# Softmax probabilities: turned by the vector engine and a trip through DRAM in place of the tensor engine, with the consumers of turned results begun later

## The chip, the cores and the metric

The kernel runs on one core of a Trainium2 chip. The core has a matrix engine (PE in the profile, with its weight loads listed apart as PEld), a vector engine (DVE), a scalar engine (ACT), GpSimd (POOL), and a queue engine, SyncE (SP), which here issues nearly every transfer between DRAM and the core's own memory (SBUF). Matrix results land in a small accumulator memory (PSUM) of eight banks. The metric is the device time of one execution in microseconds (us); the figure for a kernel is the median of several runs.

## The reference

One encoder layer on 256 tokens of width 2048, in float32, cut to what matters here:

```python
u = rmsnorm(h, norm_mix_g)
z = u @ w_in                      # split into b_a, c_a, v_a, q, k, v, gl_a, gl_b
y_a = (b_a * centred_dwconv3(c_a * v_a, conv_a_w)) @ w_out_a
q, k = rope(q), rope(k)           # 16 query heads, 4 key/value heads, head size 64
# window of +-128 tokens, one sink logit per head:
m = max(max(scores), sink); p = exp(scores - m)
p = p / (sum(p) + exp(sink - m))
y_b = (p @ v).reshape(b, s, D_ATTN) @ w_o_attn
h = h + (sigmoid(gl_a + b_a') * y_a + sigmoid(gl_b + b_b') * y_b) @ w_mix_out
up = centred_dwconv3(rmsnorm(h, norm_ffn_g) @ ffn_w_up, ffn_conv_w) + ffn_conv_b
h = h + (silu(up[..., :5632]) * up[..., 5632:]) @ ffn_w_down
out = rmsnorm(h, norm_final_g)
```

## The kernel before

**Products.** Each large product is made from rounded halves: a weight tile `raw` is cast to a high part `whi` by ACT (line 195), the rest `wlo` is a subtraction on DVE (line 206), and PE sums high and low products into one PSUM bank. The weights come in chunks of 512 KB. A product is of one of two kinds. A *single* job (lines 253 and 254) has the weights standing still and the tokens moving, and its result has features on the partitions, as the rest of the kernel wants it; a chunk is eight pairs of a 512-column and a 256-column matmul. A *quad* job (lines 229 to 231) has the tokens standing still and 512 weight columns moving, and its result has tokens on the partitions. It must be turned. `quad` (line 300) does it without PE: two DVE transposes of 32 x 32 blocks (line 310, one for each half of the tokens) into `qd`, one DMA of 512 KB to a DRAM buffer `way` (line 314), four DMAs of 128 KB back into `qf` (line 317), and then four consumers, one for each 128 features, on `qf`.

**Order of the work.** Nothing is scheduled automatically: the program order on each engine is the order in which the Python code issues. `run` walks over the chunks. At chunk c it issues the fetch of chunk c+6, the cast of chunk c+3, the subtraction of chunk c+2 and then the matmuls of chunk c; then one *step* follows. In a step every generator under way is resumed once up to its next `yield`, in the order in which they were begun, and after that the work due at this step begins (`at(n, fn)`, `later`). So a `yield 1` means "the rest is issued one chunk later", and the DVE work of the step at c stands between the subtractions of chunks c+1 and c+2. Each engine runs its own queue strictly in order, so an instruction that waits holds up all behind it. There are three `wlo` buffers, so DVE can be at most that far ahead of PE.

**Stages.** First the wide start and the single jobs of `w_in` (keys, values, queries, then the short convolution), up to about 231 us; then quad jobs for the gates, `w_oa` and `w_o` (8 pairs of rows each, so four chunks a quad), and `w_mix` (the first two of its four quads side by side). These quads live in pool `p1b`, and the code calls their setting `stage1`. Then `w_up` and `w_dn` follow in `stage2`, and four single jobs end the kernel.

**Attention** lies inside the single jobs of `w_in`, in ten blocks t = 0 to 9, at steps 29 + 21t/4. Block t issues `att_out(t - 2)`, `att_turn(t - 1, e)` for e = 0 and 1, and `att_scores(t, e)`, each as far as the first `yield`. `att_scores` puts the scores of a head for both blocks of 128 queries into banks `s0` and `s1` on PE; DVE adds the mask and takes the maximum; one step later ACT takes the exponentials into `p`; one step later DVE makes the denominator and ACT scales `p`. `att_turn` turns `p` (queries on the partitions) by four PE transposes into bank `ptp` (line 565) and, a step later, ACT copies that to `pT` (line 568). `att_out` multiplies the values `vtok` by `pT` into bank `av` (line 578). Up to block 1 the queries' rotation is also under way: `rope` moves halves with four DMAs `rot<-qkraw` (line 473) and four DMAs `two<-rcos` (line 485), all on the SP queue. `rcos` has one buffer, so the next `rcos` on DVE (line 475) waits until those DMAs have read the last one.

**Turned pairs.** `turns(which)` lets some pairs of a single job run low before high. `BEHIND` says which pairs after an attention block.

Of the kernel before, what the change touches and what calls it, by code (L numbers as in the profile page):

```python
# [7 lines left out]
F32 = mybir.dt.float32  # L8
F32R = mybir.dt.float32r
# [11 lines left out]
HD = 64  # L21
# [31 lines left out]
def hybrid_block_kernel(  # L53
    ctx: ExitStack, tc: tile.TileContext, head, wide, xT, w_in, w_gate, w_oa, w_o, w_mix, w_up, w_dn, w_end, vec, cst, out
):
    nc = tc.nc
# [4 lines left out]
    turn = ctx.enter_context(tc.tile_pool(name="turn", bufs=2, space=bass.MemoryType.DRAM))  # L61
    lin = ctx.enter_context(tc.tile_pool(name="lin", bufs=3, space=PSUM))
    aps = ctx.enter_context(tc.tile_pool(name="aps", bufs=1, space=PSUM))

    x = cpool.tile([P, KT, T], F32, tag="x", name="x")
# [55 lines left out]

    TURNS, BEHIND = (1, 5, 9, 15), {"s": (1, 5), "ptp": (1, 5), "av": (1, 4)}
    pairs = [0]
    order = {"due": None, "turned": set()}

    def turns(which=TURNS):
        order["due"], order["turned"] = which, set()
# [162 lines left out]
    S = 32  # L292

    def by_block_of_tokens(a):

        return a.rearrange("p (h a i) -> p h a i", h=2, a=4)

    under_way = [0]

    def quad(*epis, stage, bufs):  # L300
        def go(banks):
            while under_way[0] >= bufs:
                yield 1
            under_way[0] += 1
            pool = stage()
            d = pool.tile([P, 4, 2, QUAD * S], F32, tag="qd", name="qd", bufs=bufs)
            for h, ps in enumerate(banks):
                if h:
                    yield 1
                nc.vector.transpose(d[:, :, h, :], ps)  # L310
            f = pool.tile([P, 4, 2, QUAD, S], F32, tag="qf", name="qf", bufs=bufs)

            way = turn.tile([4, S, 4, 2 * QUAD * S], F32, tag="way", name="way")
            nc.sync.dma_start(way.rearrange("a j b x -> (a j) (b x)"), d.rearrange("p b h x -> p (b h x)"))
            yield 1
            for b in range(4):
                nc.sync.dma_start(  # L317
                    f[S * b : S * b + S].rearrange("p a h m i -> p a (h m i)"),
                    way[:, :, b, :].rearrange("a j x -> j a x"),
                )  # L320
            for _ in range(2):
                yield 1
            for m, epi in enumerate(epis):
                begin(epi, f[:, :, :, m, :].rearrange("p a h i -> p h a i"))
                if m < 2:
                    yield 1
            under_way[0] -= 1

        return go
# [49 lines left out]
    hd = p1.tile([P, HEAD], F32, tag="hd", name="hd")  # L379
    ct = p1.tile([P, C_END], F32, tag="ct", name="ct")  # L380
    ident = ct[:, C_ID : C_ID + P]
    hb = p1.tile([P, WIDE, P], F32, tag="hb", name="hb")


    wm = p1.tile([P, 2 * T], F32R, tag="wm", name="wm")
    nc.vector.memset(wm.bitcast(F32), 1.0)
    nc.vector.memset(ones, 1.0 / D)
    nc.vector.memset(eps, EPS)
    xs = cpool.tile([P, KT, 2 * T], F32R, tag="A", name="xs")
# [134 lines left out]
        yield 1  # L524
        nc.scalar.copy(vtok[:, :, i * P : (i + 1) * P], tp[:, :, 0:P])

    probs = {}
    mask = ct[:, C_MASK : C_MASK + T]

    def att_scores(t, e):  # L530
        kv = t // 4
        sc = aps.tile([P, 2, T], F32, tag=f"s{e}", name=f"s{e}")
        for n in range(2):
            q = qs[:, t // 2, e, t % 2, n * P : (n + 1) * P]
            nc.tensor.matmul(sc[:, n, :], q, kh[:, e, kv, :], start=True, stop=False)  # L535
            nc.tensor.matmul(sc[:, n, :], q, kl[:, e, kv, :], start=False, stop=True)  # L536
        h = PAIRS[t][e]
        sink, ns = col(V_SINK + h), nsink[:, h : h + 1]
        flat = sc.rearrange("p n t -> p (n t)")

        nc.vector.tensor_tensor(flat[:, P : 3 * P], flat[:, P : 3 * P], mask, op=ALU.add)
        st = p1.tile([P, 8], F32, tag="st", name="st", bufs=4)
        mx, nm, den, es = (st[:, 2 * i : 2 * i + 2] for i in range(4))
        nc.vector.tensor_reduce(mx, sc, axis=AX.X, op=ALU.max, negate=True)
        nc.vector.tensor_scalar(nm, mx, HD**-0.5, ns, op0=ALU.mult, op1=ALU.min)
        yield 1
        p = p1.tile([P, 2, T], F32, tag="p", name="p", bufs=3)
        for n in range(2):
            nc.scalar.activation(
                p[:, n, :], sc[:, n, :], AF.Exp, bias=nm[:, n : n + 1], scale=HD**-0.5, accum_out=den[:, n : n + 1]  # L550
            )
        nc.scalar.activation(es, nm, AF.Exp, bias=sink)
        yield 1
        nc.vector.tensor_tensor(den, den, es, op=ALU.add)
        nc.vector.reciprocal(den, den)
        for n in range(2):
            nc.scalar.mul(p[:, n, :], p[:, n, :], den[:, n : n + 1])
        probs[t, e] = p

    def att_turn(t, e):  # L560
        p = probs.pop((t, e))
        tp = aps.tile([P, 2, T], F32, tag=("tp", "tp2")[e], name="ptp")
        for b in range(2):
            for n in range(2):
                nc.tensor.transpose(tp[:, b, n * P : (n + 1) * P], p[:, n, b * P : (b + 1) * P], ident)  # L565
        yield 1
        pT = p1.tile([P, 2, T], F32, tag="pT", name="pT", bufs=2)
        nc.scalar.copy(pT, tp)
        probs[t, e] = pT

    def att_out(t):
        kv = t // 4
        o = aps.tile([P, 2 * T], F32, tag="av", name="av")
        pT = [probs.pop((t, e)) for e in range(2)]
        for b in range(2):
            for e in range(2):
                v0 = 128 * kv + 64 * e
                nc.tensor.matmul(  # L578
                    o[64 * e : 64 * e + 64, 0:T], vtok[:, b, v0 : v0 + HD], pT[e][:, b, :], start=b == 0, stop=b == 1
                )  # L580
        yield 1
        yield from split(box["B"][:, 8 + t, :], o[:, 0:T])
# [65 lines left out]
    for i in range(4):  # L648
        at(40 + 4 * i, lambda i=i: nc.sync.dma_start(x[:, 4 * i : 4 * i + 4, :], xT[:, 4 * i : 4 * i + 4, :]))


    for t in range(10):

        def block(t=t):
            if t > 1:
                begin(att_out, t - 2)
            for e in range(2):
                if 0 < t < 9:
                    begin(att_turn, t - 1, e)
            for e in range(2):  # L660
                if t < 8:
                    begin(att_scores, t, e)
            if t:
                turns(BEHIND["s" if t < 8 else "ptp" if t < 9 else "av"])

        at(29 + 21 * t // 4, block)

# [4 lines left out]
    stage1 = lambda: lazy("p1b", start_gates)  # L672
# [35 lines left out]
    def quads(w, n, rhs, epi, stage, tiles, side=1):  # L708

        jobs = []  # L710
        for q in range(len(tiles) // QUAD):
            four = [lambda f, t=t: epi(t, f) for t in tiles[QUAD * q : QUAD * q + QUAD]]
            jobs.append((w[q], n, rhs, quad(*four, stage=stage, bufs=2 if stage is stage1 else 1), "quad"))
        groups.append((2, jobs[:side], None))
        groups.extend((2, [job], None) for job in jobs[side:])

# [256 lines left out]
```

## Time and profile before

| | |
|---|---|
| median of 3 runs | 1321.75 us (1321.44 to 1321.79) |
| the profiled execution's own time | 1320.97 us |
| its span, first to last instruction | 1319.2 us |
| mean granted PE clock | 0.997 |
| PE busy | 1304.1 us, 99% of the span |
| DVE busy | 941.7 us, 71% |
| ACT busy | 678.9 us, 51% |
| POOL busy | 62.5 us, 5% |
| bytes by the DMA queues | 302.54 MB, 229 GB/s |

A row of instructions names its line, engine, operation and tiles (`ptp<-ct,p` writes `ptp` from `ct` and `p`), then the count after an x, and durations. Durations of matmuls overlap, since they are pipelined: what a matmul costs the path is the time from its start to the start of the next one. In a timeline the first number is the start in us, the second the duration, and a bracket at the end gives the engine's idle time just before and what ended it.

### The profile page before, as it was taken

What the parts mean: (1) busy time and instruction counts of PE and PEld (TensorE: products, weight loads), DVE (VectorE), ACT (ScalarE), POOL (GpSimd) and SP (SyncE); (2) the same over time, 40 slices, a digit from 0 to 9 for tenths busy, and PEclk for the clock granted to TensorE, in tenths of its full rate; (3) what the DMA queues carried; (4) which work ended last, traced back from release to release, by engine and by line L of the source; (5) the groups of instructions that cost most, each with busy time, mean ns of one, the idle gap of its engine ahead of it and who ended that gap; (6) DMA issues with size and microseconds to landing.
All of it is one profiled execution on the core that took longest, in us unless ns stands there. A gap on an engine that the chain in (4) does not pass through costs nothing.

```text
span 1319.2 us, 17559 instructions
## 1 busy us (share of the span) xinstructions
PE 1304.1 (99%) x6206; PEld 1090.2 (83%) x6206; DVE 941.7 (71%) x1390; ACT 678.9 (51%) x971; POOL 62.5 (5%) x66
## 2 busy tenths in 40 slices
PE   9999999999999999999999999999999999999997
PEld 8888888888888877878888888888888888888886
DVE  7888777555556677687798887878787875545454
ACT  7666675454444344444565555555555554434352
POOL 0000000000000000242000000000000000102031
PEclk9999999999999999999999999999999999999999
DMA  8786655677777878767776867776767676767663
GB/s 301 233 247 206 207 158 164 195 250 244 236 249 247 276 259 262 236 206 240 247 248 223 273 224 256 228 264 223 255 228 256 228 256 197 222 194 224 195 212 104
DMA packets 105032, 302.54 MB, mean 229 GB/s; under 512 B 12016, under 2 KB 35440, under 8 KB 104944
## 3 DMA queue, kind: packets, MB, share of 16 engines
q1 hardware_dynamic: 104512, 300.64, 70.7%
q8 instruction: 48, 0.79, 0.2%
q10 hardware_dynamic: 432, 0.79, 0.2%
q14 instruction: 40, 0.33, 0.1%
HBM read 271.76 MB, written 25.69 MB: 225 GB/s over the span
## 4 chain that ended last, share of the span: by engine, by line
PE 94%; DMA 3%; DVE 2%; issue 1%; SPq 0%; ACT 0%; POOLq 0%; DVEq 0%; ACTq 0%
PE pq L231 24%; PE pq L230 24%; PE pq L229 24%; PE ps L253 13%; PE ps L254 7%; DMA qf<-way 1%; DMA way<-qd 1%; DVE wlo L206 1%; PE av L578 1%; PE ptp L565 1%; SPq L317 0%; PE warm L393 0%; DVE qd L310 0%; PE s L536 0%; PE s L535 0%
## 5 line engine op out<-in xcount | busy, mean ns | idle before, releaser
L195 ACT CAST whi<-raw 128x1024 fp32r<-128x1024 f32 (+3 forms) x465 | 482.5, 1040 | 496.6 <-PE pq L230 372.9
L206 DVE TENSOR_TENSOR wlo<-raw,whi 128x1024 fp32r<-128x1024 f32 (+3 forms) x465 | 563.0, 1214 | 239.5 <-PE pq L231 134.4
L229 PE MATMUL pq<-whi,hs 128*128 128x512 f32 x704 | 274.0, 389 | 0.0
L231 PE MATMUL pq<-wlo,hs 128*128 128x512 f32 x704 | 273.9, 389 | 0.0
L230 PE MATMUL pq<-whi,hs 128*128 128x512 f32 x704 | 273.9, 389 | 0.0
L253 PE MATMUL ps<-xs,whi 128*128 128x512 f32 x576 | 200.3, 394 | 0.0
L254 PE MATMUL ps<-xs,wlo 128*128 128x256 f32 x576 | 158.0, 280 | 0.0
L229 PEld LDWEIGHTS pq<-whi,hs 128*128 128x128 f32 x704 | 132.1, 188 | 27.6
L230 PEld LDWEIGHTS pq<-whi,hs 128*128 128x128 f32 x704 | 132.1, 188 | 27.4
L231 PEld LDWEIGHTS pq<-wlo,hs 128*128 128x128 f32 x704 | 132.1, 188 | 27.3
L253 PEld LDWEIGHTS ps<-xs,whi 128*128 128x128 f32 x576 | 106.8, 188 | 22.3
L254 PEld LDWEIGHTS ps<-xs,wlo 128*128 128x128 f32 x576 | 108.9, 189 | 1.9
L229 PE MATMUL pq<-whi,xs 128*128 128x512 f32 x256 | 99.7, 390 | 0.0
L230 PE MATMUL pq<-whi,xs 128*128 128x512 f32 x256 | 99.6, 389 | 0.0
L231 PE MATMUL pq<-wlo,xs 128*128 128x512 f32 x256 | 99.6, 389 | 0.0
L458 DVE TENSOR_TENSOR evs<-qf,r 128x256 f32<-128x256 f32 x120 | 48.0, 421 | 41.8 <-DMA qf<-way 41.7
L310 DVE STREAM_TRANSPOSE qd<-pq 128x512 f32<-128x512 f32 x90 | 63.8, 709 | 9.6 <-PE pq L231 9.5
L229 PE MATMUL pq<-whi,actC 128*128 128x512 f32 x168 | 65.4, 389 | 0.0
L230 PE MATMUL pq<-whi,actC 128*128 128x512 f32 x168 | 65.4, 389 | 0.0
L231 PE MATMUL pq<-wlo,actC 128*128 128x512 f32 x168 | 65.4, 389 | 0.0
L229 PEld LDWEIGHTS pq<-whi,xs 128*128 128x128 f32 x256 | 48.0, 188 | 10.4 <-issue 0.4
L230 PEld LDWEIGHTS pq<-whi,xs 128*128 128x128 f32 x256 | 48.0, 188 | 10.0
(170 smaller groups left out, 1629.1 us busy)
## 6 DMA issues: line engine op xcount, KB each, us to landing
raw<-in_w_up_dram SPq DMA_DIRECT2D x176, 512.0 KB, 4.6
raw<-in_w_dn_dram SPq DMA_DIRECT2D x66, 512.0 KB, 4.3
raw<-in_w_gate_dram SPq DMA_DIRECT2D x64, 512.0 KB, 4.3
raw<-in_w_in_dram SPq DMA_DIRECT2D x60, 512.0 KB, 4.5
way<-qd SPq DMA_DIRECT2D x45, 512.0 KB, 2.9
qf<-way SPq DMA_DIRECT2D x180, 128.0 KB, 2.9
raw<-in_w_mix_dram SPq DMA_DIRECT2D x32, 512.0 KB, 4.5
raw<-in_w_end_dram SPq DMA_DIRECT2D x20, 512.0 KB, 3.7
```

Of the source, the lines that this page charges most:

```text
L195: nc.scalar.copy(his[c][:, a:b, :], raws[c](a, b))
L206: nc.vector.tensor_tensor(los[c][:, a:b, :], raw(a, b), his[c][:, a:b, :], op=ALU.subtract)
L229: nc.tensor.matmul(ps, ah, wh, start=k == 0, stop=False)
L230: nc.tensor.matmul(ps, al, wh, start=False, stop=False)
L231: nc.tensor.matmul(ps, ah, wl, start=False, stop=last)
L253: lambda: nc.tensor.matmul(both, hi[:, i, :], moving, start=k == 0, stop=last and turned),
L254: lambda: nc.tensor.matmul(ps[:, 0:T], lo[:, i, :], a[:, 0:T], start=False, stop=last and not turned),
L310: nc.vector.transpose(d[:, :, h, :], ps)
L458: nc.vector.tensor_tensor(by_block_of_tokens(dst), f, by_block_of_tokens(rr["r"]), op=ALU.mult)
L565: nc.tensor.transpose(tp[:, b, n * P : (n + 1) * P], p[:, n, b * P : (b + 1) * P], ident)
L578: nc.tensor.matmul(o[64 * e : 64 * e + 64, 0:T], vtok[:, b, v0 : v0 + HD], pT[e][:, b, :], start=b == 0, stop=b == 1)
```

## The change

Four things change; the numbers of matmuls and of weight bytes stay.

1. `att_turn` goes. In `att_scores`, a step after `p` is scaled, DVE turns its 32 x 32 blocks into a tile `pd` (for both heads of block t, four instructions of 128 x 256); then, as in `quad`, one DMA of 512 KB goes to `way` and, a step later, four DMAs of 128 KB come back into `pT`. `att_out` reads `pT` with runs of 32 elements. The trip that `quad` had inline is now the function `by_dram` that both use.
2. `quad` waits a number of steps between the reads and the first consumer: it was 2 everywhere, and is 4 in `stage1` (with 3 buffers in place of 2) and 3 in `stage2`.
3. The turned pairs: block 0 gets `TURNS`, block 1 none, block 8 the setting of "av".
4. To make room, `hb` shares the place of `pd` and the warm-up tile that of `p`, and `p` has two buffers, not three.

```diff
-    TURNS, BEHIND = (1, 5, 9, 15), {"s": (1, 5), "ptp": (1, 5), "av": (1, 4)}
+    TURNS, BEHIND = (1, 5, 9, 15), {"s": (1, 5), "av": (1, 4)}
...
+    def by_dram(dst, src):
+        way = turn.tile([4, S, 4, src.shape[-1] // 4], F32, tag="way", name="way")
+        nc.sync.dma_start(way.rearrange("a j b x -> (a j) (b x)"), src)
+        yield 1
+        for b in range(4):
+            nc.sync.dma_start(dst[S * b : S * b + S], way[:, :, b, :].rearrange("a j x -> j a x"))
...
-    def quad(*epis, stage, bufs):
+    def quad(*epis, stage, bufs, wait):
...
-            for _ in range(2):
+            yield from by_dram(f.rearrange("p a h m i -> p a (h m i)"), d.rearrange("p b h x -> p (b h x)"))
+            for _ in range(wait):
                 yield 1
...
-        p = p1.tile([P, 2, T], F32, tag="p", name="p", bufs=3)
+        p = p1.tile([P, 2, T], F32, tag="p", name="p", bufs=2)
...
-        probs[t, e] = p
-    def att_turn(t, e):
-        p = probs.pop((t, e))
-        tp = aps.tile([P, 2, T], F32, tag=("tp", "tp2")[e], name="ptp")
-        for b in range(2):
-            for n in range(2):
-                nc.tensor.transpose(tp[:, b, n * P : (n + 1) * P], p[:, n, b * P : (b + 1) * P], ident)
-        yield 1
-        pT = p1.tile([P, 2, T], F32, tag="pT", name="pT", bufs=2)
-        nc.scalar.copy(pT, tp)
-        probs[t, e] = pT
+        yield 1
+        if e == 0:
+            d = p1.tile([P, CH, P], F32, tag="pd", name="pd").rearrange("p k f -> p (k f)")
+            trips[t] = d.rearrange("p (b e n k i) -> p b e n k i", b=4, e=2, n=2, k=2)
+        d = trips[t]
+        for n in range(2):
+            nc.vector.transpose(d[:, :, e, n].rearrange("p b k i -> p k b i"), p[:, n, :])
+        if e == 0:
+            return
+        f = p1.tile([P, 4, 2, 2, 2, S], F32, tag="pT", name="pT", bufs=2)
+        yield from by_dram(f.rearrange("p a e n k i -> p a (e n k i)"), d.rearrange("p b e n k i -> p (b e n k i)"))
+        probs[t] = f
...
             for e in range(2):
-                if 0 < t < 9:
-                    begin(att_turn, t - 1, e)
-            for e in range(2):
                 if t < 8:
                     begin(att_scores, t, e)
-            if t:
-                turns(BEHIND["s" if t < 8 else "ptp" if t < 9 else "av"])
+            if t != 1:
+                turns(BEHIND["s" if t < 8 else "av"] if t else TURNS)
...
+        flow = {"bufs": 3, "wait": 4} if stage is stage1 else {"bufs": 1, "wait": 3}
...
-            jobs.append((w[q], n, rhs, quad(*four, stage=stage, bufs=2 if stage is stage1 else 1), "quad"))
+            jobs.append((w[q], n, rhs, quad(*four, stage=stage, **flow), "quad"))
```

Three places in the programs show what moves. On PE, at block 2, the end of one chunk, then the block: `av` the attention product, `ptp` the transposes, `s` the scores, and the next chunk of a single job. Before:

```order
L253 MATMUL ps<-xs,whi 128x512
L254 MATMUL ps<-xs,wlo 128x256
L578 MATMUL av<-pT,vtok 64x256 x4
L565 MATMUL ptp<-ct,p 128x128 x8
L535 MATMUL s_1305<-kh,qs 128x256
L536 MATMUL s_1305<-kl,qs 128x256
```

After, at the same place:

```order
L253 MATMUL ps<-xs,whi 128x512
L254 MATMUL ps<-xs,wlo 128x256
L584 MATMUL av<-pT,vtok 64x256 x4
L540 MATMUL s_1305<-kh,qs 128x256
L541 MATMUL s_1305<-kl,qs 128x256
```

The eight `ptp` rows are gone and nothing stands in their place.

On SP, around blocks 0 and 1, where the last two rotations of queries are under way (`raw` is a weight chunk). Before:

```order
L180 DMA raw<-in_w_in_dram 128x1024 x3
L485 DMA two<-rcos 64x512 x4
L180 DMA raw<-in_w_in_dram 128x1024
L473 DMA rot<-qkraw 32x512 x4
L180 DMA raw<-in_w_in_dram 128x1024 x3
L485 DMA two<-rcos 64x512 x4
```

After:

```order
L180 DMA raw<-in_w_in_dram 128x1024 x2
L304 DMA way<-pd 128x1024
L180 DMA raw<-in_w_in_dram 128x1024
L490 DMA two<-rcos 64x512 x4
L307 DMA pT<-way 32x4x256 x4
L180 DMA raw<-in_w_in_dram 128x1024
L478 DMA rot<-qkraw 32x512 x4
L180 DMA raw<-in_w_in_dram 128x1024 x3
L490 DMA two<-rcos 64x512 x4
```

The trip's write and one weight fetch now stand ahead of `two<-rcos`, and the trip's four reads ahead of `rot<-qkraw`. On DVE the four transposes of block 0 stand right before them, behind the sum that `two<-rcos` carries away.

On DVE, in `w_mix`, where the results of the first two quads are added to `x` and split into `hs` (`qd` is the drain of a quad's banks). Before:

```order
L206 TENSOR_TENSOR wlo<-raw,whi 128x1024 x2
L699 TENSOR_TENSOR x<-x,qf 128x256
L206 TENSOR_TENSOR wlo<-raw,whi 128x1024
L699 TENSOR_TENSOR x<-x,qf 128x256 x2
L206 TENSOR_TENSOR wlo<-raw,whi 128x1024
L699 TENSOR_TENSOR x<-x,qf 128x256 x3
L279 SCALAR_TENSOR_TENSOR hs<-x,vt,hs 128x256
L206 TENSOR_TENSOR wlo<-raw,whi 128x1024
L699 TENSOR_TENSOR x<-x,qf 128x256 x2
L279 SCALAR_TENSOR_TENSOR hs<-x,vt,hs 128x256 x2
L206 TENSOR_TENSOR wlo<-raw,whi 128x1024
```

After:

```order
L206 TENSOR_TENSOR wlo<-raw,whi 128x1024 x4
L701 TENSOR_TENSOR x<-x,qf 128x256
L206 TENSOR_TENSOR wlo<-raw,whi 128x1024
L701 TENSOR_TENSOR x<-x,qf 128x256 x2
L206 TENSOR_TENSOR wlo<-raw,whi 128x1024
L701 TENSOR_TENSOR x<-x,qf 128x256 x3
L279 SCALAR_TENSOR_TENSOR hs<-x,vt,hs 128x256
L206 TENSOR_TENSOR wlo<-raw,whi 128x1024
L701 TENSOR_TENSOR x<-x,qf 128x256 x2
L279 SCALAR_TENSOR_TENSOR hs<-x,vt,hs 128x256 x2
L321 STREAM_TRANSPOSE qd<-pq 128x4x128
L206 TENSOR_TENSOR wlo<-raw,whi 128x1024
```

The first addition stands two subtractions later, and the drain of the third quad now falls inside the group.

More of the change, by code (lines that the diff above doesn't have):

```diff
@@ L311, in go @@
             f = pool.tile([P, 4, 2, QUAD, S], F32, tag="qf", name="qf", bufs=bufs)
-            way = turn.tile([4, S, 4, 2 * QUAD * S], F32, tag="way", name="way")
-            nc.sync.dma_start(way.rearrange("a j b x -> (a j) (b x)"), d.rearrange("p b h x -> p (b h x)"))
-            yield 1
[L316 to L320, printed above, removed]
-            for _ in range(2):
+            yield from by_dram(f.rearrange("p a h m i -> p a (h m i)"), d.rearrange("p b h x -> p (b h x)"))
+            for _ in range(wait):
                 yield 1
@@ L381, in hybrid_block_kernel @@
     ident = ct[:, C_ID : C_ID + P]
-    hb = p1.tile([P, WIDE, P], F32, tag="hb", name="hb")
-    wm = p1.tile([P, 2 * T], F32R, tag="wm", name="wm")
-    nc.vector.memset(wm.bitcast(F32), 1.0)
+    hb = p1.tile([P, CH, P], F32, tag="pd", name="hb")[:, 0:WIDE, :]
+    wm = p1.tile([P, 2, T], F32, tag="p", name="wm", bufs=2).rearrange("p n t -> p (n t)")
+    nc.vector.memset(wm, 1.0)
+    wm = wm.bitcast(F32R)
     nc.vector.memset(ones, 1.0 / D)
@@ L525, in epi_v @@
         nc.scalar.copy(vtok[:, :, i * P : (i + 1) * P], tp[:, :, 0:P])
-    probs = {}
+    probs, trips = {}, {}
     mask = ct[:, C_MASK : C_MASK + T]
@@ L573, in att_out @@
         o = aps.tile([P, 2 * T], F32, tag="av", name="av")
-        pT = [probs.pop((t, e)) for e in range(2)]
+        pT = probs.pop(t).rearrange("p a e n k i -> p e k n a i")
         for b in range(2):
@@ L578, in att_out @@
                 nc.tensor.matmul(
-                    o[64 * e : 64 * e + 64, 0:T], vtok[:, b, v0 : v0 + HD], pT[e][:, b, :], start=b == 0, stop=b == 1
+                    o[64 * e : 64 * e + 64, 0:T], vtok[:, b, v0 : v0 + HD], pT[:, e, b], start=b == 0, stop=b == 1
                 )
```

## The prediction

> **What bounds the kernel now.** I read the page's busy shares and the chain that ended last first, then busy time by stretches, then the waits, then timelines of the places that the change touches.
>
> ```profile
> PE 1304.1 (99%) x6206; PEld 1090.2 (83%) x6206; DVE 941.7 (71%) x1390; ACT 678.9 (51%) x971; POOL 62.5 (5%) x66
> ...
> PE 94%; DMA 3%; DVE 2%; issue 1%; SPq 0%; ACT 0%; POOLq 0%; DVEq 0%; ACTq 0%
> ```
>
> PE is busy nearly throughout and is 94% of the chain. So work taken from PE shortens the kernel, work given to others is free while they keep ahead, and the only other thing to win is time in which PE waits. Where does it wait? Busy time by stretches, PE alone (first the stretch and its length, then PE busy and its instructions, the granted clock, DMA share, GB/s):
>
> ```profile
> 475.00:570.00 95.00, 90.06 (x382) 0.98 0.72 236
> 570.00:1220.00 650.00, 650.00 (x2869) 1.00 0.73 236
> ```
>
> From 570 to 1220 us a matmul takes 650/2869 = 0.2266 us and PE never stops. From 475 to 570 us 382 of them should take 86.6 us and take 95.0: 8.4 us are lost there, in `w_o` and `w_mix`. The waits tell to what:
>
> ```profile
> PE pq L231 <- DVE wlo L206: 4.9, 5, 1.9
> ...
> PEld pq L231 <- DVE wlo L206: 8.2, 9, 2.3
> ...
> DVE gates L690 <- DMA qf<-way: 10.3, 4, 4.3
> ...
> DVE x L699 <- DMA qf<-way: 10.6, 3, 3.9
> ...
> DVE evs L458 <- DMA qf<-way: 41.7, 28, 3.9
> ```
>
> PE waits for `wlo`, and DVE makes it late because it stands in front of a consumer whose `qf` has not landed. The 41.7 us of the last row belong to gates and `w_up`, where DVE has room and PE does not wait.
>
> **Part A, the PE transposes go.** Blocks 1 and 2 on PE:
>
> ```profile
> 92.14 1.04 PE L565 MATMUL ptp<-ct,p 128*128 128x128 f32 x8
> ...
> 92.93 0.36 PE L535 MATMUL s<-kh,qs 128*128 128x256 f32 x1
> ...
> 107.97 1.08 PE L578 MATMUL av<-pT,vtok 128*64 128x256 f32 x8
> 108.98 1.09 PE L565 MATMUL ptp<-ct,p 128*128 128x128 f32 x8
> 109.83 0.36 PE L535 MATMUL s<-kh,qs 128*128 128x256 f32 x1
> ```
>
> Start to start, the eight transposes cost 0.79 us in block 1 and 0.85 us in block 2; blocks 3 to 8 have the same eight. 0.79 + 7 x 0.85 = 6.7 us on the path. The slower first matmul of another type (0.36 us) stays where `av` comes before, so I count nothing for it.
>
> ```profile
> L565 PE MATMUL ptp<-ct,p x64: 272/273/329, 92.1 to 216.7; 128*128 128x128 f32 x64
> ```
>
> The Trainium skill, "TensorE: Matmul & The Clock Gate", Part 4 (PE-mode transpose), gives about 275 ns for a transpose in a kernel; the row's 273 ns agrees as a duration. Taken as a price it would make 64 x 0.273 = 17.5 us; the starts above say 0.106 each, and they decide.
>
> The 16 ACT copies go too; ACT is not waited for there, so that is worth nothing.
>
> **Part B, the turned pairs.** Chunk starts after block 0, and after block 1:
>
> ```profile
> 83.66 0.40 PE L253 MATMUL ps<-xs,whi 128*128 128x512 f32 x1
> ...
> 86.49 0.40 PE L253 MATMUL ps<-xs,whi 128*128 128x512 f32 x1
> ...
> 99.55 0.39 PE L253 MATMUL ps<-xs,whi 128*128 128x512 f32 x1
> ...
> 102.33 0.39 PE L253 MATMUL ps<-xs,whi 128*128 128x512 f32 x1
> ```
>
> Eight pairs take 2.83 us where no pair was turned after a block, 2.78 us where some were. Block 0 now gets turns, block 1 loses them: 5 chunks x 0.05 = 0.25 us won and the like lost. I take 0, ends plus and minus 0.3.
>
> **Part C, DVE and SP get the turning.** A transpose of 128 x 256 from SBUF is not in the trace; the nearest is twice the size, from PSUM:
>
> ```profile
> L310 DVE STREAM_TRANSPOSE qd<-pq 128x512 f32<-128x512 f32 x90 | 63.8, 709 | 9.6 <-PE pq L231 9.5
> ...
> way<-qd SPq DMA_DIRECT2D x45, 512.0 KB, 2.9
> qf<-way SPq DMA_DIRECT2D x180, 128.0 KB, 2.9
> ...
> 144.50:161.40 16.90, 13.05 (x26) 1.00 0.51 170
> 161.40:178.30 16.90, 12.88 (x26) 1.00 0.55 179
> ```
>
> Half of 709 ns: about 0.36 us, 1.45 us for the four of a block; ends 0.36 (size alone) and 0.71 (the writes go in runs of 32). From block 3 on (the last two rows are DVE's busy time) DVE idles 3.9 to 4.0 us a block, so this is covered, even with a block 0.85 us shorter. The trip takes 2.9 + four issues + 2.9 us, under 10 us. It starts three steps after the scores and its user comes ten steps after them, over 16 us later, so PE does not wait for `pT`. Its 8 MB are 3% more bytes, in a stage where the DMA engines are half busy.
>
> The place without room is 88 to 123 us, where the rotation of queries is under way. DVE and SP there, and PE's need for chunk 38's and 43's `wlo`:
>
> ```profile
> 87.94 0.69 DVE L481 TENSOR_TENSOR rcos<-rcos,rot 128x512 f32<-128x512 f32 x1
> ...
> 93.04 0.76 DVE L475 TENSOR_TENSOR rcos<-qkraw,ct 128x256 f32<-128x256 f32 x2 [1.80 <-DMA two<-rcos]
> ...
> 96.36 1.22 DVE L206 TENSOR_TENSOR wlo<-raw,whi 128x1024 fp32r<-128x1024 f32 x1
> ...
> 103.24 1.22 DVE L206 TENSOR_TENSOR wlo<-raw,whi 128x1024 fp32r<-128x1024 f32 x1
> ...
> 110.59 0.43 DVE L541 TENSOR_TENSOR s<-s,ct 128x256 f32<-128x256 f32 x1 [0.56 <-PE s L536]
> ...
> 119.97 1.22 DVE L206 TENSOR_TENSOR wlo<-raw,whi 128x1024 fp32r<-128x1024 f32 x1
> ...
> 88.70 2.43 SPq L485 DMA_DIRECT2D two<-rcos  x4
> ...
> 105.10 0.39 PE L253 MATMUL ps<-xs,whi 128*128 128x512 f32 x1
> ...
> 122.23 0.28 PE L254 MATMUL ps<-xs,wlo 128*128 128x256 f32 x1
> ```
>
> DVE waits 1.80 us until `two<-rcos` has read `rcos`. That DMA starts at 88.70, when the sum is done. Now the four transposes (1.45), then the issue of `way` and of a weight chunk (about 0.8) come in front: it starts near 90.95, so the next `rcos` starts at 95.3, not 93.04, and all DVE work behind it is 2.25 us late. Queued behind: the mask of block 1 and `wlo` of chunk 36, ready at 99.8 (97.58 + 2.25), while PE, 0.79 us earlier by part A, wants it at 99.0 (99.55 + 0.23 - 0.79). PE waits 0.9. Chunk 38: ready 106.7, wanted at 105.33 + 0.1: another 1.3. Block 1's own transposes then add 1.45, against idle time of 0.56 and some on ACT; chunk 43 is ready near 123.4 (121.19 + 2.3) and wanted at 122.8 (block 2 is 0.85 shorter): another 0.7. Sum 2.9 us lost. After that DVE waits for PE before block 3 and is level again. Bounds: if `two<-rcos` is not held up, the 1.80 us cover the transposes of block 0, and only chunk 43 is late: 0.8. If the DMA also lands a microsecond later behind the two transfers of 512 KB ahead of it: 5.
>
> **Part D, consumers begin later.** In `w_o`, DVE alone:
>
> ```profile
> 475.00:516.00 41.00, 34.55 (x62) 1.00 0.77 258
> ```
>
> Of 41.0 us DVE works 34.55; the other 6.45 it mostly waits for `qf`. Two more steps are 5.4 us and more than the longest of these waits, 4.3. Without them its work fits, and PE's losses there go. In `w_mix` both first quads end together, and their results come in one burst:
>
> ```profile
> 554.48 0.43 DVE L699 TENSOR_TENSOR x<-x,qf 128x256 f32<-128x256 f32 x1 [3.86 <-DMA qf<-way]
> ...
> 559.23 1.63 DVE L206 TENSOR_TENSOR wlo<-raw,whi 128x1024 fp32r<-128x1024 f32 x1
> ...
> 564.04 1.75 DVE L206 TENSOR_TENSOR wlo<-raw,whi 128x1024 fp32r<-128x1024 f32 x1
> ...
> 560.92 0.50 PE L231 MATMUL pq<-wlo,ms 128*128 128x512 f32 x1 [0.62 <-DVE wlo L206]
> ...
> 565.85 0.50 PE L231 MATMUL pq<-wlo,ms 128*128 128x512 f32 x1 [1.92 <-DVE wlo L206]
> ...
> 567.35 0.63 PE L229 MATMUL pq<-whi,ms 128*128 128x512 f32 x1
> ```
>
> DVE loses 3.86 us, then PE 0.62 and 1.92, then several matmuls run at half speed (0.63 us long). Without the wait DVE could begin the burst about 3 us earlier (the three `wlo` buffers hold it back), which covers the 2.54; but two drains of 0.71 us now fall into the burst. So I leave 1.8 us lost, ends 0 and 3.9 (2.54 + 1.4). Part D wins 8.4 - 1.8 = 6.6.
>
> "TensorE: Matmul & The Clock Gate" of the Trainium skill, Why this matters for your kernels, has the clock fall back only after idle gaps over some 3 us. Here it fell after 0.62 and 1.92; by that rule what is left costs its own length alone, by the trace it may bring slow matmuls again.
>
> In `stage2` three steps for two change nothing on PE: it never waits there (650.00 of 650.00), and a quad under way for seven steps still ends before the next one, eight chunks later. More buffers and shared places cost nothing: the sharers are used at the start, tens of us apart.
>
> **The sum.** -6.7 + 0 + 2.9 - 6.6 = -10.4 us on the profiled execution's 1320.97 us: 1310.6. The median of the runs stands 0.8 above that execution, so 1311.3. Less than 0.2% (2.6 us) could not be told from no change.
>
> **The rivals.**
> - *Attention is not held up.* For it: the 1.80 us idle, and ACT freed of its copies. Against it: SP's order. C is 0.8 and the burst fits: 1307.4 to 1309.2.
> - *The stalls at 475 to 570 us are DVE's work, not its wait.* For it: `w_o` keeps DVE 84% busy, and the burst is work. Then D wins 1.5, and 1316.4 comes out. Against it: PE's losses follow the rows that wait for `qf`.
> - *`av` slows on `pT`'s runs of 32.* No row has such a moving operand, so nothing excludes it. `av` takes 1.01 us a block start to start (107.97 to 108.98), some 0.85 of it streaming; at half speed eight blocks cost 6.8 more: 1318.1. Against it: nothing in the trace but that contiguous operands of all sizes run at one rate.
> - *Slower: DVE becomes the bound of the attention.* The transposes write in runs of 32. Cover is 4.0 - 0.85 = 3.15 us a block; to eat A and D (13.3) the loss must be 1.7 a block, so four transposes of 4.9 us, 1.2 each. At 1.6 each: 8 x (6.4 - 3.15) = 26, and 1334. Against it: 0.71 for twice the size.
>
> That the change does not take place is ruled out: the rows `ptp` are gone from PE's order.
>
> **How the numbers follow.** My forecast 45% (1308.5 to 1314 by the bounds of C and D); first rival 23%, second 14%, third 8%, slower 4%; 6% for mixtures, such as pairs in the slow order after every block (8 x 0.25 = 2 us). The range 1307 to 1317 leaves out some of the first rival, the third and the fourth: 2 in 10. Faster 0.91 (all but the last rival and a worse third one), same 0.05, slower 0.04.
>
> **What would show it.** A: no `ptp`, and `av` followed by `s` after about 1.0 us. C: `rcos` waiting for `two<-rcos` until about 95, PE waiting for `wlo` near 99, 105 and 122. D: the waits of DVE for `qf` under 10 us in all, PE without gaps from 475 to 550 us, at most 4 us lost near 560. It is wrong if a transpose of DVE takes over 0.7 us, if `av` grows, or if PE still waits in `w_o`.

## The result, and the profile after

| | before | changed |
|---|---|---|
| median | 1321.60 us (1319.94 to 1321.79, 4 runs) | 1313.84 us (1312.64 to 1313.97, 4 runs) |
| ratio | | 0.9942, 95% interval 0.9925 to 0.9959 |
| profiled execution | 1320.97 us, span 1319.2 us | 1313.97 us, span 1312.1 us |

The row of the kernel before has one run more than the table ahead of the prediction. The kernel became 0.6% faster: 7.8 us by the medians, 7.0 us between the two profiled executions. That is the forecast's direction, inside its range, and 2.5 us above the 1311.3 that it named.

The busy shares and the chain of the changed kernel, from its page:

```profile
PE 1297.1 (99%) x6142; PEld 1084.6 (83%) x6142; DVE 950.6 (72%) x1422; ACT 668.2 (51%) x955; POOL 55.2 (4%) x66
...
PE 98%; DVE 1%; DMA 0%; ACT 0%; SPq 0%; issue 0%; POOLq 0%; DVEq 0%; ACTq 0%
```

PE has 64 instructions fewer (6206 before; the transposes are counted among its matmuls), DVE 32 more, ACT 16 fewer. PE is now 98% of the chain that ended last (94% before). This share alone says little: it is 96% in e1 below, which is faster still.

Where did the 7 us come from? Three starts on PE cut the program into stages: the first scores, the first matmul behind the attention (`pq` on `xs`), and the first of the last group (`more`). The timeline of PE, before (start, duration):

```profile
77.05 0.28 PE L535 MATMUL s<-kh,qs 128*128 128x256 f32 x1
...
231.83 0.50 PE L229 MATMUL pq<-whi,xs 128*128 128x512 f32 x1
...
1304.04 0.40 PE L790 MATMUL more<-actA,last 128*128 128x256 f32 x2
```

and of the changed kernel:

```profile
77.73 0.28 PE L540 MATMUL s<-kh,qs 128*128 128x256 f32 x1
...
231.63 0.50 PE L229 MATMUL pq<-whi,xs 128*128 128x512 f32 x1
...
1296.95 1.96 PE L793 MATMUL more<-actA,last 128*128 128x256 f32 x15
```

The attention takes 153.90 us where it took 154.78: only 0.9 us won, though PE lost 64 instructions there. From its end to `more` it is 1065.3 us against 1072.2: 6.9 us won. The remaining 0.7 us were lost ahead of the first scores, which start anywhere from 76.4 to 77.7 us in the runs below, whatever was changed. So nearly the whole gain is the longer waits, and the attention gave back what it won. The waits of the changed kernel (who waited for whom, us in total, times, longest):

```profile
PE ps L254 <- DVE wlo L206: 3.7, 1, 3.7
...
PE pq L231 <- DVE wlo L206: 1.2, 2, 0.8
...
DVE rcos L480 <- DMA two<-rcos: 8.0, 2, 5.8
...
DVE evs L463 <- DMA qf<-way: 2.5, 3, 1.1
DVE wlo L206 <- DMA qf<-way: 1.5, 1, 1.5
```

DVE's waits for `qf`, 75 us in all before, are down to 4.0. PE has a new wait, 3.7 us for `wlo`, and behind it stands one of DVE: 5.8 us for the transfer `two<-rcos` (2.1 at most before). The place, first on PE, with the busy time of the stretch behind the wait (its last three columns are granted clock, DMA share and GB/s):

```profile
99.15 0.39 PE L253 MATMUL ps<-xs,whi 128*128 128x512 f32 x1
103.22 0.58 PE L254 MATMUL ps<-xs,wlo 128*128 128x256 f32 x1 [3.69 <-DVE wlo L206]
103.60 0.63 PE L253 MATMUL ps<-xs,whi 128*128 128x512 f32 x1
...
106.16 0.54 PE L253 MATMUL ps<-xs,whi 128*128 128x512 f32 x1
106.54 0.28 PE L254 MATMUL ps<-xs,wlo 128*128 128x256 f32 x1
```

```profile
103.20:106.50 3.30, 3.28 (x10) 2.88 (x11) 3.19 (x6) 1.10 (x2) 0.00 (x0) 0.51 0.78 248
```

The gap is 4.07 us start to start where a matmul of this kind takes 0.23: 3.84 lost. Then five pairs run at about half speed (the granted clock is 0.51, and the long matmul takes 0.63 us instead of 0.39), and take 3.32 us from 103.22 to 106.54 where five pairs take 5 x 0.347 = 1.73: 1.6 more. One stop costs 5.4 us; of the stops that the forecast named near 105 and 122 us there is none. Why DVE came late, on DVE and on SP:

```profile
88.80 1.42 DVE L570 STREAM_TRANSPOSE pd<-p 128x256 f32<-128x256 f32 x4
...
98.63 0.76 DVE L480 TENSOR_TENSOR rcos<-qkraw,ct 128x256 f32<-128x256 f32 x2 [5.84 <-DMA two<-rcos]
...
101.95 1.22 DVE L206 TENSOR_TENSOR wlo<-raw,whi 128x1024 fp32r<-128x1024 f32 x1
```

```profile
84.12 0.33 SPq L180 DMA_DIRECT2D raw<-in_w_in_dram  x1
90.25 0.33 SPq L304 DMA_DIRECT2D way<-pd  x1
90.67 0.38 SPq L180 DMA_DIRECT2D raw<-in_w_in_dram  x1
91.14 2.70 SPq L490 DMA_DIRECT2D two<-rcos  x4
```

SP issues a weight chunk at 84.12 and then nothing until 90.25: it stands at block 0's `way`, which waits for the four transposes of DVE. The weight chunk of 90.67 and `two<-rcos` are queued behind it. The forecast had the start of `two<-rcos` right (90.95; it is 91.14), but the next `rcos`, expected at 95.3, starts at 98.63. (The forecasts count on the timeline of the kernel before; in the measured starts 0.7 us is the later start of the scores.)

### The profile page after: what moved, and what is told of

Same layout as the page of the kernel before. It is cut to its first block, busy times and chain, and to the rows that moved or that the text cites. A ratio compares the mean times of both kernels' runs of the same rounds, so it can differ in the third digit from the quotient of the medians.

```text
span 1312.1 us, 17495 instructions
## 1 busy us (share of the span) xinstructions
PE 1297.1 (99%) x6142; PEld 1084.6 (83%) x6142; DVE 950.6 (72%) x1422; ACT 668.2 (51%) x955; POOL 55.2 (4%) x66
## 4 chain that ended last, share of the span: by engine, by line
PE 98%; DVE 1%; DMA 0%; ACT 0%; SPq 0%; issue 0%; POOLq 0%; DVEq 0%; ACTq 0%
PE pq L231 26%; PE pq L229 26%; PE pq L230 25%; PE ps L253 12%; PE ps L254 7%; PE av L584 1%; DMA two<-rcos 0%; PE warm L398 0%; PE s L540 0%; DVE wlo L206 0%; PE s L541 0%; SPq L490 0%; PE more L793 0%; DVE st L549 0%; POOLq L971 0%
## 5 line engine op out<-in xcount | busy, mean ns | idle before, releaser
L229 PEld LDWEIGHTS pq<-whi,xs 128*128 128x128 f32 x256 | 48.1, 188 | 10.4 <-issue 0.4
L231 PEld LDWEIGHTS pq<-wlo,xs 128*128 128x128 f32 x256 | 48.1, 188 | 10.1
```

Of the source, the lines that this page charges most:

```text
L229: nc.tensor.matmul(ps, ah, wh, start=k == 0, stop=False)
L231: nc.tensor.matmul(ps, ah, wl, start=False, stop=last)
```

## The experiments

A kernel is compared with the kernel before on the same chip; that one's median is 1319.86 us beside e1 to e4, 1317.92 beside e5 to e8, 1318.24 beside e9 and e10, 1319.73 beside e11 and 1320.81 beside e12. So it moves by a few us from chip to chip, and small differences are read from the traces.

**The first question: is it the place of `way` in SP's queue?** In e1 block 0 issues `way` two steps later, behind `two<-rcos`:

```
         d = trips[t]
         ...
         if e == 0:
             return
+        for _ in range(2 if t == 0 else 0):
+            yield 1
         f = p1.tile([P, 4, 2, 2, 2, S], F32, tag="pT", name="pT", bufs=2)
```

> The changed kernel, with the DMA write of block 0 (way<-pd) issued two steps later, so that two<-rcos stands ahead of it on SP again; the DVE transposes stay where they are. Theory (two<-rcos is held up in the queues behind 1 MB of way and weights, DVE waits for it until 98.6, PE until 103.0): rcos starts near 93, the 3.8 us gap of PE and its half-speed matmuls near 99 to 107 us go, 4.5 to 5.5 us are won on the changed kernel: 1308.4 to 1309.4. Rival 1 (the four DVE transposes of 1.42 us in front of it make the gap): the gap stays, 1313.8. Rival 2 (DMA load as such: the trip's bytes slow all transfers of that stretch, whatever the order): the gap moves to chunk 38 or 43 and at most 2 us are won: 1312.

Measured: 1307.85 us (1306.92 to 1308.56), ratio 0.9913 (0.9899 to 0.9926), 6.0 us under the changed kernel by the medians and 5.9 by the spans. The timelines of SP and DVE in e1:

```profile
84.05 2.31 SPq L180 DMA_DIRECT2D raw<-in_w_in_dram  x2
88.88 2.54 SPq L490 DMA_DIRECT2D two<-rcos  x4
```

```profile
93.32 0.76 DVE L480 TENSOR_TENSOR rcos<-qkraw,ct 128x256 f32<-128x256 f32 x2 [0.60 <-DVE wlo L206]
```

`rcos` starts 5.3 us earlier. It still waits 0.60 us, and that for the transfer: the row names DVE's own subtraction, which was done before the wait began, while the last part of `two<-rcos` was issued at 90.8 and landed 2.3 us later. The gap of PE is gone, and the attention takes 148.5 us (77.53 to 226.01). Its cost beside part A is down to some 0.4 us.

In e3 nothing is delayed, but block 0's write goes out on another queue:

```
-        nc.sync.dma_start(way.rearrange("a j b x -> (a j) (b x)"), src)
+        (queue or nc.sync).dma_start(way.rearrange("a j b x -> (a j) (b x)"), src)
...
+            nc.scalar if t == 0 else nc.sync,
```

> The changed kernel, with the DMA write of block 0 issued from ACT's queue at the same step, so that SP's queue has only one weight chunk ahead of two<-rcos. Theory 1 (the place in SP's queue decides): two<-rcos is issued near 89.5, lands near 93, and the gap of PE goes: 1308.5 to 1309.5. Theory 2 (the bytes ahead of it on the same DMA engines decide, whichever queue they came from): it is issued near 89.5 but lands at 96 or later, and the gap shrinks by about the earlier issue, 1.5 to 2.5 us: 1311 to 1312.5.

Measured: 1309.21 us (1308.64 to 1312.77), ratio 0.9929 (0.9913 to 0.9946). `two<-rcos` starts at 88.42 and the long gap is gone; there is one of 1 us later, at the chunk that the forecast had second. So it is SP's order that delays the start. What the bytes ahead do, e3 doesn't tell, since `way` went out at 89.72, behind the start of `two<-rcos`; and now ACT stands 3.49 us, until the transposes are done. Both runs come out near where the prediction's first rival stood, in which the attention is not held up (1307.4 to 1309.2); counted from the kernel before beside them they win 12.0 and 10.7 us, a little less than that rival's 12.6 to 14.4.

**The other half alone.** e2 is the kernel before with only the longer waits, e4 the changed kernel with only the old ones:

```
 e2, in the kernel before:
-            for _ in range(2):
+            for _ in range(wait):
 ...
+        flow = {"bufs": 3, "wait": 4} if stage is stage1 else {"bufs": 1, "wait": 3}
 e4, in the changed kernel:
-        flow = {"bufs": 3, "wait": 4} if stage is stage1 else {"bufs": 1, "wait": 3}
+        flow = {"bufs": 2, "wait": 2} if stage is stage1 else {"bufs": 1, "wait": 2}
```

> The kernel before with the longer waits of quad alone (4 steps and 3 buffers in stage1, 3 steps in stage2), attention untouched. Theory (the gain of the change is nearly all from here, the attention wins and loses about the same): 6.9 us won on the kernel before, within 0.5 us: about 1314.5, that is as fast as the whole change within 1 us. PE without gaps from 475 to 555 us and about 2 us lost in w_mix. Rival (the waits need the time that the attention part frees): under 4 us won, 1317.5 or more.

> The changed kernel with the old waits of quad (2 steps everywhere, 2 buffers in stage1). Theory (attention wins 6.7 by the transposes and loses 5.5 to 6 near 99 us and at 126 us, net about 0): 1320.5 to 1321.5, no different from the kernel before, with PE's gaps of 8 us back from 475 to 570 us. Rival (the longer waits did not matter): 1314.

Measured: e2 1314.75 us (1314.09 to 1315.27), ratio 0.9965 (0.9952 to 0.9979); e4 1322.01 us (1320.60 to 1324.41), ratio 1.0019 (1.0011 to 1.0028). The longer waits carry the gain, and the new way of turning, as it stands, costs a little. By the medians e2 wins 5.1 us, between the 6.9 expected and its rival's 4; by its profile's stage from the attention to `more` it wins 6.7. PE's stretch from 475 to 570 us in e2 and in the changed kernel:

```profile
475.00:570.00 95.00, 93.64 (x413) 76.87 (x412) 73.23 (x108) 44.57 (x59) 13.43 (x15) 1.00 0.75 249
```

```profile
475.00:516.00 41.00, 41.00 (x182) 33.97 (x181) 36.46 (x65) 21.00 (x32) 0.00 (x0) 1.00 0.84 289
475.00:570.00 95.00, 93.78 (x413) 77.02 (x412) 73.94 (x108) 44.50 (x59) 13.26 (x15) 1.00 0.73 243
```

Both have 413 matmuls there where the kernel before had 382: 31 x 0.2266 = 7.0 us. In `w_o` (475 to 516 us) PE is now busy all the time, and DVE works 36.46 us instead of 34.55.

The differences of e2 and e4 from the kernel before beside them add up to -3.0 us, not to -7.8. So the changed kernel was run once more, on another chip:

> The changed kernel itself once more, because the two halves alone (longer waits -5.1 us, attention +2.2 us against the kernel before beside them) add up to -2.9 us and the whole change gave -7.8 us on another chip. Theory (the halves are independent and the difference is how much the kernel before loses in its stalls from chip to chip, 1316 to 1322 us): 1312 to 1315 here, with the gap of 3 to 4 us near 99 us, and a ratio of 0.994 to 0.997. Rival (the two halves help each other: the shorter attention does something for the stalls at 475 to 570 us): a ratio of 0.9942 or less again.

Measured: 1314.36 us (1313.33 to 1314.49), ratio 0.9947 (0.9933 to 0.9961), 6.5 us under the kernel before beside it. The gap near 99 us is there again, and longer:

```profile
104.04 0.58 PE L254 MATMUL ps<-xs,wlo 128*128 128x256 f32 x1 [5.29 <-DVE wlo L206]
```

By the stages of the profiled executions the halves do add up, to about a microsecond and a half: the attention takes 154.8 us in e2 and 155.3 in e4 (154.8 before, 153.9 after), the part from it to `more` 1065.5 and 1071.5 (1072.2 before, 1065.3 after). What the medians have beyond that may lie in how long the stalls of each kernel are from run to run, since this one gap is 3.7 us in one profile and 5.3 in the other; it is not shown, and which part of the 5 us that would be is left open.

**What makes `two<-rcos` land late?** It starts 2.4 us later than before, yet `rcos` comes 5.6 us later (0.7 of both is the later start of the scores). In e9 and e10, `way` goes late as in e1, and a copy of `pd` that nobody reads is written at the old place:

```
+        if t == 0:
+            aside = turn.tile([P, CH * P], F32, tag="aside", name="aside")      # e9: [P, 2 * P]
+            nc.sync.dma_start(aside, d...)                                      # e9: d...[:, 0 : 2 * P]
         for _ in range(2 if t == 0 else 0):
```

> The kernel of e1_way_later, with one more DMA on SP at the place where the changed kernel writes block 0's way: it copies a quarter of pd (128 KB, 1 KB from each partition) to a tile that nobody reads. It has to wait for the four transposes, as way has, so two<-rcos starts near 91 again; only the bytes ahead of it are 384 KB fewer. Theory (the start, 2.4 us late, and the bytes ahead, 3 us of landing, each make a part of the changed kernel's loss of 6 us): rcos starts at 96.0 to 97.0 rather than 98.6, PE waits 1 to 2 us near 99, and the time is 1309 to 1310.5. Rival A (the place in SP's queue is all): rcos at 98 or later and 1313 to 1314. Rival B (the bytes are all): rcos by 95 and 1308 to 1308.5.

> As e9_quarter_ahead, with all 512 KB of pd copied to the tile that nobody reads, at the place where the changed kernel writes way; way itself still goes two steps later. Theory: the changed kernel's loss is back: two<-rcos starts near 91, rcos near 98.6, one gap of PE of 3 to 4 us near 99 with matmuls at half speed behind it, and 1313 to 1314.5. Rival (it was the early start of the trip's reads or of what follows, not what stands ahead of two<-rcos): within 1 us of 1307.85.

Measured: e9 1313.72 us (1311.90 to 1314.29), ratio 0.9966 (0.9953 to 0.9979); e10 1314.63 us (1311.96 to 1315.37), ratio 0.9971 (0.9960 to 0.9983). A quarter of the bytes costs as much as all of them. The theory that the bytes of `way` make a part was wrong; rival A, the place in the queue, is what came. DVE in e9:

```profile
97.93 0.76 DVE L480 TENSOR_TENSOR rcos<-qkraw,ct 128x256 f32<-128x256 f32 x2 [6.04 <-DMA two<-rcos]
```

What else stands in that queue is the weight chunk. The DMA engines' share and GB/s (last two columns) around the wait, in the changed kernel and then in e1:

```profile
84.50:88.00 3.50, 3.50 (x21) 3.06 (x21) 3.46 (x7) 3.37 (x8) 0.00 (x0) 1.00 0.64 218
88.00:90.50 2.50, 2.50 (x16) 2.19 (x15) 2.46 (x7) 1.17 (x2) 0.00 (x0) 1.00 0.02 8
```

```profile
84.50:88.00 3.50, 3.50 (x22) 3.08 (x22) 3.46 (x7) 3.50 (x8) 0.00 (x0) 1.00 0.91 297
88.00:90.50 2.50, 2.50 (x16) 2.21 (x15) 2.46 (x7) 1.17 (x2) 0.00 (x0) 1.00 0.66 224
```

While SP waits at `way`, nothing is issued, and the DMA engines run empty: 8 GB/s from 88.0 to 90.5 us against 224. The chunk that e1 (and the kernel before) moves in that time is issued at 90.67 instead, just ahead of `two<-rcos`. It takes 5.7 us to land, and the four parts of `two<-rcos` right behind it take 5.4, where they take 2.3 in e1 and before the change:

```profile
two<-rcos SPq DMA_DIRECT2D x4, 128.0 KB, 5.4
```

e11 undoes this alone: the same copy of all of `pd`, directly before `two<-rcos` and behind the chunk.

```
 in rope, before the DMAs of two:
+        if 0 in trips and "aside" not in trips:
+            trips["aside"] = turn.tile([P, CH * P], F32, tag="aside", name="aside")
+            nc.sync.dma_start(trips["aside"], trips[0]...)
```

> As e10_whole_ahead, but the copy of all 512 KB of pd to the tile that nobody reads is issued directly before two<-rcos, behind the weight chunk, not ahead of both. SP still waits at it for the four transposes, until about 90.2; the weight chunk, though, starts near 86 again, while the transposes are still to come. Theory now (e9 showed that the copy's bytes don't matter: what is left of the loss is the weight chunk of 512 KB that the wait holds back and lets start only just ahead of two<-rcos): rcos starts at 95 to 96, PE waits 0.5 to 1.5 us near 99 and as much near 105, and the time is 1308.5 to 1310.5. Rival (SP's wait alone makes it, wherever the chunk stands): rcos at 97.5 or later, a gap of 3 us or more near 99, 1312.5 to 1314.5.

Measured: 1310.72 us (1309.82 to 1311.91), ratio 0.9932 (0.9915 to 0.9950), 0.2 us above the expected times. SP, the transfer's time to landing, and then DVE, in e11:

```profile
83.15 3.62 SPq L180 DMA_DIRECT2D raw<-in_w_in_dram  x3
90.59 0.33 SPq L490 DMA_DIRECT2D aside<-pd  x1
91.01 2.50 SPq L493 DMA_DIRECT2D two<-rcos  x4
```

```profile
two<-rcos SPq DMA_DIRECT2D x4, 128.0 KB, 2.9
```

```profile
95.83 0.76 DVE L480 TENSOR_TENSOR rcos<-qkraw,ct 128x256 f32<-128x256 f32 x2 [2.70 <-DMA two<-rcos]
```

`two<-rcos` starts as late as in the changed kernel (91.01), with 512 KB of the copy ahead of it, and `rcos` still starts 2.8 us earlier, at 95.83. PE stops twice, 1.14 us at 99 and 1.12 at 106 us, and no matmul behind them is slow. So the loss has two parts, which the attention's time in the profiles tells (148.5 us in e1, 151.2 in e11, 153.9 in the changed kernel). `two<-rcos` waits for the transposes: 2.7 us, with the copy's bytes in it, behind which `two<-rcos` lands in 2.9 us and not 2.3. And the weight chunk waits with it and gets in front: another 2.7 us, of which 1.6 are the slow matmuls. The medians, from different chips, say 2.9 and 3.1.

**Has DVE room for more transposes?** e5 is e1 with each transpose done twice:

```
         for n in range(2):
-            nc.vector.transpose(d[:, :, e, n]..., p[:, n, :])
+            for _ in range(2):
+                nc.vector.transpose(d[:, :, e, n]..., p[:, n, :])
```

> The kernel of e1_way_later, with DVE's four transposes of each block done twice: 32 more transposes at 0.36 us start to start, 1.4 us of DVE work more a block, 11.4 us in all. Theory (this work is covered from block 3 on, where DVE idles about 3 us a block; only the rotation at 88 to 123 us has no room): 1308.5 to 1310, at most 2 us above e1_way_later's 1307.85, all of it before 125 us. Rival (DVE is close to being the bound of the attention): its work shows one to one, 1315 to 1319.

Measured: 1315.12 us (1313.55 to 1316.68), ratio 0.9976 (0.9967 to 0.9986), 7.3 us above e1. The expected cost of at most 2 us was wrong, and so was the place: the loss reaches to 150 us. DVE's busy time (third busy column) in e5:

```profile
88.00:106.00 18.00, 17.08 (x102) 14.86 (x100) 17.48 (x36) 8.55 (x20) 0.00 (x0) 1.00 0.79 230
106.00:125.00 19.00, 17.50 (x100) 14.21 (x101) 18.36 (x39) 13.63 (x31) 0.00 (x0) 1.00 0.81 258
125.00:144.00 19.00, 18.43 (x110) 15.46 (x108) 18.38 (x41) 11.05 (x24) 0.00 (x0) 1.00 0.68 233
161.00:178.00 17.00, 17.00 (x102) 14.32 (x101) 16.45 (x36) 11.98 (x28) 0.00 (x0) 1.00 0.69 224
```

and the first three stretches in e1:

```profile
88.00:106.00 18.00, 18.00 (x107) 15.78 (x106) 17.01 (x36) 9.64 (x23) 0.00 (x0) 1.00 0.88 256
106.00:125.00 19.00, 18.91 (x114) 15.33 (x112) 18.49 (x39) 14.84 (x31) 0.00 (x0) 1.00 0.82 267
125.00:144.00 19.00, 19.00 (x115) 16.25 (x114) 16.89 (x33) 11.93 (x27) 0.00 (x0) 1.00 0.75 259
```

From 161 us on a block takes it all: DVE at 16.45 of 17.00, PE never waiting. Up to 125 us DVE was already full in e1 (17.01 of 18.00, then 18.49 of 19.00). What is added there, and still stands in front of it up to 144 us, comes out on PE nearly one to one (four times 1.4 us are added by then): five waits for `wlo`, 4.7 us in all, the last of them with matmuls at half speed behind it:

```profile
145.67 0.39 PE L254 MATMUL ps<-xs,wlo 128*128 128x256 f32 x1 [2.25 <-DVE wlo L206]
...
147.46 0.63 PE L253 MATMUL ps<-xs,whi 128*128 128x512 f32 x1
```

Of the 8.1 us between the spans of e5 and e1 (1314.3 and 1306.2), 7.1 have come together when block 4's scores start, at 151.0 us. The last one is no wait: behind that stop the pairs run at 0.352 to 0.354 us in most chunks where they take 0.347 in e1, in the same program order.

**What are the PE transposes worth?** e7 is e1 with eight transposes of a constant before the scores of blocks 1 to 8, whose result nobody reads:

```
+            for e in range(2):
+                if 0 < t < 9:
+                    tp = aps.tile([P, 2, T], F32, tag=("tp", "tp2")[e], name="ptp")
+                    for n in range(4):
+                        nc.tensor.transpose(tp[:, n // 2, n % 2 * P : n % 2 * P + P], ident, ident)
```

> The kernel of e1_way_later, with eight PE transposes of a constant 128 x 128 tile before the scores of blocks 1 to 8, whose result nobody reads: the removed work of PE alone, without the copies, without its wait for probabilities. Theory (part A's term, read start to start): 8 x 0.85 = 6.8 us more, 1314.3 to 1315. Rival (a transpose costs its whole duration of 0.273 us): 64 x 0.273 = 17.5 us more, 1325. Second rival (part A's term was covered by other waits): under 2 us more, 1308 to 1310.

Measured: 1313.42 us (1312.98 to 1314.34), ratio 0.9969 (0.9958 to 0.9981): 5.6 us above e1 by the medians, which are from different chips, and 6.3 by the profiled executions (1314.34 and 1308.08); the attention takes 154.9 us and not 148.5. That is a little less than the 6.8 expected. In its trace a block's eight stand on the path with 0.84 us, from their first start to the scores:

```profile
146.01 1.09 PE L668 MATMUL ptp<-ct 128*128 128x128 f32 x8
146.85 0.36 PE L540 MATMUL s<-kh,qs 128*128 128x256 f32 x1
```

Their whole durations (64 x 0.273 = 17.5) are out.

**What is left, and the turned pairs.** e6 is e1 with a quad's four results handed on one in each step of the first stage (before, the last two in one):

```
-                if m < 2:
+                if m < (2 if wait == 3 else QUAD):
                     yield 1
```

> The kernel of e1_way_later, with the four results of a quad of the first stage handed on one in each step, not two in the first two steps and the last two in one. Theory (what is left of the stall in w_mix, 1.7 us, is a burst of DVE work): the two gaps of PE near 560 us shrink below 0.5 us in all, and the time is 1306.0 to 1307.0. Rival (they come from the three wlo buffers or from the data's arrival): within 0.4 us of 1307.85, with the gaps where they are.

Measured: 1306.60 us (1306.13 to 1306.98), ratio 0.9917 (0.9900 to 0.9933), the fastest version here: 1.2 us under e1, and 1.1 under e8 below, which ran beside it. One wait of 0.48 us is left of the two in `w_mix`. By the starts of the matmuls e1 loses 1.5 us there and e6 0.8. So about half of the rest was the burst; what makes the other part was not tried. Of the 1.5 us between the spans of e1 and e6 the other 0.75 lie ahead of the quad jobs, where the two programs are the same.

e8 is e1 with the pairs turned as before, none at block 0:

```
-            if t != 1:
-                turns(BEHIND["s" if t < 8 else "av"] if t else TURNS)
+            if t:
+                turns(BEHIND["s" if t < 8 else "av"])
```

> The kernel of e1_way_later, with pairs turned as before: none at block 0, after the scores of block 1. Theory (part B is worth 0, a gain of 0.25 us after block 0 and the like loss after block 1): the pairs after block 0 run at 0.354 us each and those after block 1 at 0.347, and the time is within 0.6 us of e1_way_later's 1307.85. Rival (the turns at block 0 carry some of the gain): over 1 us slower.

Measured: 1307.69 us in one run, which shows no difference to e1. By its matmul starts the pairs behind block 0 take 0.353 to 0.354 us, as foreseen, but those behind block 1 do as well (0.352 to 0.354), not 0.347; from its first scores to the end of the attention it takes 149.0 us where e1 takes 148.5. Whether pairs run at the one rate or the other depends on more than the turns, as e5 showed too.

## Why the prediction was right, and which term was off

- **What bounds the kernel**: held. PE is the path, and nearly all that was won is time in which it had waited.
- **Part A, -6.7 us**: held. From `s` to `s`, block 4 to 5, it is 16.07 us (149.48 to 165.55) and was 16.89 (146.40 to 163.29): 0.82 a block. Putting transposes back costs 0.84 a block. `av` is followed by `s` after 1.02 us, as foreseen.
- **Part B, 0**: small, but not as reasoned. By the one trace of e8 the new turns win 0.6 us of the attention, beyond the bounds of 0.3: what was to be lost behind block 1 was not, since the pairs run at 0.347 to 0.348 there in e1, though none is turned.
- **The transposes of DVE**: the four take 1.42 us (1.45 foreseen), 0.404 us each with the next begun before the end.
- **Part C, +2.9 us**: the mis-sized term. The attention won 0.9 in all, so with 6.7 won by A, C cost 5.8. The step that failed is "so the next `rcos` starts at 95.3": it counted the issue of `way` and of a weight chunk (0.8 us) in front of `two<-rcos`, and let the transfer then take its old time. But the chunk had been held back by the same wait, while the DMA engines ran empty, so its 512 KB came in front too, and `two<-rcos` took 5.4 us to land and not 2.3. e11 is close to what the term had in mind, a start of `two<-rcos` near 91 and little else: `rcos` at 95.83, stops of 1.14 and 1.12 us at the two first places named (none at the third), and an attention 3.1 us above what part A alone would leave, where 2.9 was said. The stated upper bound of 5, a landing one microsecond later, was short by nearly one: `rcos` came 3.3 us later than forecast (2.6 without the later start of the scores), and the slow matmuls behind a long stop (1.6) were not in the sum.
- **Part D, -6.6 us**: held, -6.9. `w_o` has no stall left, and `w_mix` keeps two waits, 0.47 and 0.75 us by their rows; with the matmuls behind them these are 1.8 us by the starts, as many as were left in the sum. Whether the two drains make them was not tried; spreading the results (e6) takes away about half of what e1 keeps.
- **The sum**: -10.4 foreseen, -7.0 between the profiled executions; C explains 2.9 of the 3.4, the start ahead of the first scores 0.7, and D gave 0.3 more than foreseen.
- **The rivals.** The first, attention not held up, did not happen, but e1 shows it, at 1307.85 and 12.0 us under the kernel before beside it (1307.4 to 1309.2, or 12.6 to 14.4, was said). That the stalls are DVE's work and not its wait falls with `w_o`: DVE does more there in the same time and PE does not stop. That `av` slows on runs of 32 falls with its row:

```profile
L584 PE MATMUL av<-pT,vtok x64: 379/379/431, 113.0 to 231.3; 128*64 128x256 f32 x64
...
L570 DVE STREAM_TRANSPOSE pd<-p x32: 400/404/441, 88.8 to 207.6; 128x256 f32<-128x256 f32 x32
```

  0.379 us, unchanged. DVE as the bound of all the attention falls: a transpose at 0.404 us, 0.35 start to start, is far from the 1.2 that it needed. But e5 shows how near that bound lies in the first blocks: twice the transposes cost 7.3 us, nearly all of it ahead of 151 us.
- **The clock.** The Trainium skill, "TensorE: Matmul & The Clock Gate", Why this matters for your kernels, lets the clock fall only behind idle gaps of more than about 3 us. The stop of 3.69 us here was followed by slow matmuls, which agrees; the stops of 0.47 and 0.75 us were not. Between, the runs decide otherwise: in e5 a wait of 2.25 us was followed by them 1.4 us later. In e4 one of 1.92 us, with 1.05 before it, was not, while in the kernel before the same 1.92, with 0.62 before it, was. The rows of e4:

```profile
561.59 0.50 PE L231 MATMUL pq<-wlo,ms 128*128 128x512 f32 x1 [1.05 <-DVE wlo L206]
566.52 0.50 PE L231 MATMUL pq<-wlo,ms 128*128 128x512 f32 x1 [1.92 <-DVE wlo L206]
```

  So about 2 us goes either way here; what decides it was not tried.

## What to carry to other kernels

A DMA that has to wait for a compute engine stops its whole queue: look at what the queue would have issued during the wait, and count those transfers in front of whatever comes behind it, not only their issue. Move such a DMA behind the ones that are already free to go, or to another engine's queue, which then waits in its place (ACT, 3.49 us in e3); here two steps' delay of one transfer was worth 6 us, nearly as much as the change itself. And an engine's idle time covers added work only in the stage where it idles: in e5 the added transposes cost 7.1 us up to block 4, where four times 1.4 were added, and of the 8.1 us only 1.0 came behind it.

## What was not expected of the hardware

- The DMA engines moved 8 GB/s for 2.5 us, in a stage at 200 to 300 GB/s, because one issuing engine stood at one wait.
- The bytes directly ahead mattered less than which transfer they were: 128 KB or 512 KB of the copy ahead of the chunk gave `rcos` at 97.93 and 98.04, the weight chunk of 512 KB moved out from between gave 95.83. Issued behind the wait, the chunk took 5.7 to 6.8 us to land (the changed kernel, e9, e10, e12); the copy took 1.7 us with 128 KB and 2.9 to 3.0 with 512. Why 512 KB of the one take so much longer than of the other was not tried.
- A transpose of DVE of 128x256 in float32, SBUF to SBUF, took 0.404 us, 0.35 start to start; eight PE transposes of 128x128 took 0.84 us start to start, though each row is 0.27 long.
- Matmuls at half speed came behind a stop of 2.25 us (granted clock 0.5 from 147.1 us on), and did not behind two of 1.14 and 1.12 us seven microseconds apart.
